# A distance table repeated from memory to memory between weight tiles, and narrow columns loaded apart from the stream

## The chip, the cores and the metric

The kernel runs on one core of one Trainium2 chip. The metric is the device time of one execution in microseconds (us), as the median of several runs. All times below come from one profiled execution of the kernel before, except where "runs" are named. Engines are PE (matrix multiply), ACT, DVE and POOL (elementwise work), SP (which only issues transfers here), and 16 DMA engines that all queues share.

## The reference

Two transformer blocks in float32 on 256 tokens of width 2048, one after the other. The first block has modulated attention, pooling and a feed-forward of width 8192. The second has four attention branches, a gate for each, and an output projection. What matters here is the end of the first block and the start of the second:

```python
hm = modulate(rms_norm(x, norm_mlp_w), sh_m, sc_m)
x = x + g_m * squared_relu_mlp(hm, w_mlp_up, w_mlp_down)   # feed-forward
...
h = rms_norm_2(x, norm_w)
p = h @ w_in                       # (2048, 17492)
(z, gate, dsa_qkv, idx_q, idx_k, idx_w, fox_qkv, fox_f, diff_qkv, dil_qkv) = jnp.split(p, IN_OFFSETS, axis=-1)
bias_dsa, bias_diff, bias_dil = jnp.split(rel_bias, 3, axis=-1)   # rel_bias: (32, 12)
...
bias = bias_table[t5_bucket(tq[:, None] - key_pos[None, :])].transpose(2, 0, 1)
logits = jnp.where(causal, logits + bias[None, :, None], -jnp.inf)
```

Three of the branches add a bias to their logits that depends only on the distance of query and key and on the head: 3 branches of 4 heads, 12 rows in all. `idx_k` (64 columns), `idx_w` (16) and `fox_f` (4) are the narrow columns of `p`: 84 of them, of which 80 lie side by side.

## The kernel before, in words

**Weights as a stream.** Every weight is read once, in tiles of 1 MB (512 rows by 512 columns). The order is written out by hand as a list of items (L278 to L381). `issue` (L127) takes the next item, finds a free buffer `raw` (three of them, and two more up to the second quarter of the feed-forward, L396) and starts its transfer on SP's queue (L148). What `with_issue` holds for an item is called just before that item's own transfer (L142). `prep` (L157) splits half a tile at a time: ACT rounds it to `wh` (L65, called from L172) and DVE forms the rest `wl` (L68). There are five buffers of each. `take` (L222) hands a half-tile to PE and lets `prep` run three half-tiles ahead. When both halves of a tile are split, its buffer is free and the next transfer is issued. PE does three products for each step of 128 rows and each half of the tokens (L231 to L233): 12 for a half-tile.

**Small work in between.** After each half-tile `tick` (L94) takes one step of the queue `hp` and, by `lp_rate`, steps of the queue `lp`. These are generators with the small work of the stage: transposes, norms, attention.

**Feed-forward.** Four quarters `c` (L1003). Each has 16 tiles of `w_mlp_up` and then 16 of `w_mlp_down`. Beside the up tiles of `c` = 1 and 2 run 12 tiles of `w_ada` that DVE multiplies and sums into `g_part` (L177 to L190), and no `lp` work is left in this stage. The item of the first down tile of `c` = 1 is `down_blk[1, 0][0]`, and the 16 down items have numbers that follow each other.

**Between the blocks.** The pool `b1` of the first block is closed and `b2` is opened at the same place in memory (L1043 to L1046). A tile of `b2` waits only for the tiles of `b1` whose bytes it takes (`reuse_waits="tile"`). The first tiles of `b1` were `crows` (512 bytes of each partition) and the two extra `raw` buffers (8 KB each). The second of these became `g_part`, which is read to the end of the feed-forward. The other carries weights for the last time in `c` = 0. A tile with tag `T` of `b2` takes 4 KB, and there are two.

On POOL's queue then come, in this order: the factor of the norm (L485), four pieces of the norm's row (L1052), the table `c2`, `relb`, `bucket_hot` and `dist_mask` (the last two into a `T` tile `hv`), and seven small transfers (L1092 to L1099). `tables` (L1103), a generator in `hp`, multiplies `relb` by `hot` on PE (L1105), adds the mask on DVE (L1107) and issues one transfer on POOL's queue: 12 rows of 383 numbers, in 12 partitions, each written 128 times to `dist_bias` in memory (L1108). `bias_tile` (L1122) later reads from there, for each branch, rows that are shifted by one from partition to partition. This runs beside the projection of the first branch (`qkv("dsa")`).

**The narrow columns** are item `sm` of the stream (L370), after the tiles of the first branch: one item of 16 steps of 128 rows by 84 columns, fetched by two transfers into one `raw` buffer, in pieces of 320 and of 16 bytes. PE uses it at L1472 to L1474.

```python
it = items[i]
if i in with_issue:
    with_issue.pop(i)()
if it[0] == "w":
    ...
    for src, c0, c1 in parts:
        nc.sync.dma_start(v[:, :, c0:c1], src.rearrange("(k p) n -> p k n", p=128))
```

Of the kernel before, what the change touches and what calls it, by code (L numbers as in the profile page):

```python
# [17 lines left out]
T = 256  # L18
# [4 lines left out]
# tiles of weights on their way: always, and more in the first block  # L23
RAW, RAW_EXTRA = 3, 2
# where the second input is loaded in the order of the weights
CTX_AT = "u0"
# tiles of the modulation: before the feed-forward, in the input projection, beside each half of the output projection
FILL, ADA_IN, ADA_POOL, ADA_REST = 4, 10, 4, 1
# background steps beside the output projection; steps by which queries and keys are turned later than they are projected
LP1, LAG, LAGK = 1.1, 3, 2  # L30
# background steps beside each branch of the second block
RATES = (1.2, 1.2, 1.2, 1.0)

# columns of the constant table of the first block
C1_COS, C1_SIN, C1_SEL, C1_N = 0, 128, 256, 258
# columns of the constant table of the second block
C2_TRI, C2_CNT, C2_CAUSAL, C2_SCORE, C2_N = 0, 256, 512, 768, 1024
# columns of the second block's input projection
# [4 lines left out]
def two_blocks_kernel(ctx: ExitStack, tc: tile.TileContext, I, out: bass.AP):  # L43
# [83 lines left out]
    def issue():  # L127
        i = state["issued"]
        if i >= len(items):
            return  # L130
        if i < extra["until"] and extra["live"] < RAW_EXTRA:
            extra["live"] += 1
            from_extra.add(i)
            r = extra["pool"].tile([128, 2048], FP32, tag="raw", name="raw", bufs=RAW_EXTRA)
        elif extra["main"] < RAW:
            extra["main"] += 1
            r = raw_p.tile([128, 2048], FP32, tag="raw", name="raw")
        else:
            return
        state["issued"] += 1  # L140
# [4 lines that stand above are left out]
            _, parts, kt, n = it  # L145
            v = r[:, 0:kt * n].rearrange("p (k n) -> p k n", k=kt)
            for src, c0, c1 in parts:
                nc.sync.dma_start(v[:, :, c0:c1], src.rearrange("(k p) n -> p k n", p=128))  # L148
            raws[i] = v
        elif it[0] == "ak":  # L150
            raws[i] = r[:, 0:4 * it[3].shape[1]].rearrange("p (k n) -> p k n", k=4)
            nc.sync.dma_start(raws[i], it[3].rearrange("(k p) n -> p k n", p=128))
        else:
            raws[i] = r.rearrange("p (k n) -> p k n", k=4)
            nc.sync.dma_start(r, it[3])

    def prep():  # L157
# [8 lines left out]
        if it[0] == "w":  # L166
# [4 lines left out]
            src = r[:, h * kh:(h + 1) * kh, :]  # L171
# [5 lines left out]
        elif it[0] == "av":  # L177
            # this part's share of the row, by partition
            _, key, k, _ = it
            rf = r.rearrange("p k n -> p (k n)")  # L180
            c = cst[:, k, 0:1]
            if not g_part:
                g_part.append(extra["pool"].tile([128, 2048], FP32, tag="raw", name="g_part", bufs=RAW_EXTRA))
                V.tensor_scalar(g_part[0], rf, c, None, op0=OP.mult)
            else:
                for h_ in range(2):
                    s_ = slice(1024 * h_, 1024 * h_ + 1024)
                    V.scalar_tensor_tensor(out=g_part[0][:, s_], in0=rf[:, s_], scalar=c, in1=g_part[0][:, s_],
                                           op0=OP.mult, op1=OP.add)
            done = True  # L190
        else:
            # four products at a time, each in 32 columns of the array
            kind, key, k, _ = it
            n_k = 4 if kind == "ak" else FILL if key == ("g", 5) else 16
            n = r.shape[2]
            if k == 0:
                accs[key] = bank([128, n], "adab", "ada")
            for j in range(4):
                PE.matmul(out=accs[key][32 * j:32 * j + 32, :], lhsT=cst[:, 4 * k + j if kind == "ak" else k, :],  # L199
                          rhs=r[:, j, :], start=k == 0, stop=k == n_k - 1)  # L200
            if k == n_k - 1:
                rows = b1.tile([128, 512], FP32, tag="rows", name="rows", bufs=2)[:, 0:n]
                act(rows, accs.pop(key))
                after_item[key[0]](rows, *key[1:])
            done = True
        if done:
            raws.pop(i)
            extra["live" if i in from_extra else "main"] -= 1
            issue()
# [77 lines left out]
    # groups of the rows of w_in, in steps of 128; the first are short for an early start  # L287
# [55 lines left out]
    # two blocks of columns, whose groups of rows come in an order of their own  # L343
# [23 lines left out]
    for nm, c0, nb in (("dsa", DSA0, 3), ("sm", 0, 0), ("idx", IDXQ0, 2), ("fox", FOX0, 3), ("diff", DIFF0, 3),  # L367
                       ("dil", DIL0, 3), ("z", Z0, 4)):
        if nm == "sm":
            in2["sm"] = [add_w("w", [(w_in2[:, IDXK0:IDXK0 + 80], 0, 80), (w_in2[:, FOXF0:FOXF0 + 4], 80, 84)], 16, 84)]  # L370
        else:
            if nm == "dsa":
                in2["dsa", 0] = pair_w(w_in2, 0, c0, c0 + 512, LATE)
            for j in range(2 if nm == "dsa" else 0, nb):
                in2[nm, j] = w_block(w_in2, 0, c0 + 512 * j)
# [53 lines left out]
    # bias of the gates of the residual, in the rows where their products land  # L429
# [17 lines left out]
    # silu of both conditions, the stationary operand of the modulation  # L447
# [33 lines left out]
    # reciprocal root of the mean of squares  # L481
# [36 lines left out]
    # scaled per partition, split in two parts  # L518
# [4 lines left out]
    # scaled and shifted per column, split in two parts  # L523
# [125 lines left out]
    # turned by the position, in place but for the last sum; each head twice, side by side  # L649
# [127 lines left out]
    # a unit: one head, half of the tokens; two heads of the same tokens follow each other  # L777
# [93 lines left out]
    # rows of the pooling branch, beside the attention  # L871
# [24 lines left out]
    # rows of the attention  # L896
# [40 lines left out]
    hm_hi, hm_lo = [], []  # L937

    # the norm's factor of each token, in all partitions
# [61 lines left out]

    fh = lhs_of(hm_hi, hm_lo)
    for c in range(4):  # L1003
        if c == 1:
            V.tensor_tensor(out=gb[5], in0=g_rows[5], in1=gb[5], op=OP.add)
# [41 lines left out]

    def wt(shape, name="w"):
# [35 lines left out]
    relb = b2.tile([32, 12], FP32, name="relb", bufs=1)  # L1084
    G.dma_start(relb, I["rel_bias_2"])
    hv = b2.tile([128, 2, 512], FP32, tag="T", name="hv")
    hot, vmask = hv[:, 0], hv[:, 1]
    G.dma_start(hot[0:32, 0:384], I["bucket_hot"])
    G.dma_start(vmask[0:12, 0:384], I["dist_mask"])
# [10 lines left out]
    dist_bias = dram.tile([12, 128, 383], FP32, name="dist_bias")  # L1100
    lam = b2.tile([128, 4], FP32, name="lam", bufs=1)

    def tables():  # L1103
        bk = bank([128, 384], "bias")
        PE.matmul(out=bk[0:12, :], lhsT=relb, rhs=hot[0:32, 0:384], start=True, stop=True)  # L1105
        vec = vmask[0:12, 0:384]
        V.tensor_tensor(out=vec, in0=bk[0:12, :], in1=vec, op=OP.add)  # L1107
        G.dma_start(dist_bias, bc(vec[:, None, 0:383], [12, 128, 383]))  # L1108
        yield
# [73 lines left out]
    # names: attention whose operands must be gone first  # L1183
# [137 lines left out]
    def fox(f_nat):  # L1321
# [8 lines left out]
        # log(1 + u) = 2 artanh(u / (2 + u))  # L1330
# [44 lines left out]
    def diff():  # L1375
# [32 lines left out]
        def sixth(u, pt):  # L1408
# [4 lines left out]
            # a sum of squares past the largest float32 makes the reference's reciprocal root 0  # L1413
# [51 lines left out]
    # few columns: the weights stand still, the tokens move  # L1465
# [144 lines left out]
    # the last rows of the last block: one half of the tokens first  # L1610
# [22 lines left out]
def _constants():  # L1633
# [9 lines left out]
    # keys of the other block: within 128 positions, or far below any score  # L1643
# [28 lines left out]
    # distance 255 - m in column m  # L1672
# [32 lines left out]
```

## Time and profile before

| | |
|---|---|
| runs (3) | median 2212.37 us, 2210.87 to 2212.54 |
| profiled execution, first to last instruction (span) | 2209.1 us |
| what lies around the span | 3.3 us, by the median; the page gives no time of its own for the profiled execution |
| PE busy | 2141.7 us, 97% |
| DVE, ACT, POOL busy | 55%, 44%, 1% |
| read and written by DMA | 468.9 MB, 212 GB/s on average |
| granted clock of PE | 0.987 of full speed on average |

Every row of the trace has its start in us from the first instruction. A row of a chain or a timeline gives the start, how long it took, the engine and line, and `output<-input`. Brackets give how long the engine had been idle before it and what released it. A matmul's own time (0.39 us) is longer than its share of PE's time, because the next one starts before it ends; the distance of two starts is what counts. "DMA share" is the mean busy share of the 16 DMA engines; q1 is the queue of SP's transfers and q0 that of POOL's.

### The profile page before, as it was taken

What the parts mean: (1) busy time and instruction counts of PE and PEld (TensorE: products, weight loads), DVE (VectorE), ACT (ScalarE), POOL (GpSimd) and SP (SyncE); (2) the same over time, 40 slices, a digit from 0 to 9 for tenths busy, and PEclk for the clock granted to TensorE, in tenths of its full rate; (3) what the DMA queues carried; (4) which work ended last, traced back from release to release, by engine and by line L of the source; (5) the groups of instructions that cost most, each with busy time, mean ns of one, the idle gap of its engine ahead of it and who ended that gap; (6) DMA issues with size and microseconds to landing.
All of it is one profiled execution on the core that took longest, in us unless ns stands there. A gap on an engine that the chain in (4) does not pass through costs nothing.

```text
span 2209.1 us, 25697 instructions
## 1 busy us (share of the span) xinstructions
PE 2141.7 (97%) x10291; PEld 1694.4 (77%) x10291; DVE 1220.0 (55%) x1552; ACT 973.4 (44%) x1355; POOL 33.0 (1%) x59
## 2 busy tenths in 40 slices
PE   6899999999999999999999889999999999999998
PEld 3566655678888888888888777888888888888886
DVE  2455655555546646554456447756665555555554
ACT  4433344355444434434444444445544444444443
POOL 1000000000000000000001000000000000000000
PEclk8999999999999999999999999999999999999999
DMA  9988876665547667556545764444546555555553
GB/s 332 325 313 335 316 285 235 236 226 195 202 160 279 229 208 249 193 188 198 183 153 190 187 216 153 162 170 155 181 169 214 197 189 196 189 197 189 193 191 114
DMA packets 215703, 468.90 MB, mean 212 GB/s; under 512 B 12472, under 2 KB 21148, under 8 KB 206624
## 3 DMA queue, kind: packets, MB, share of 16 engines
q1 hardware_dynamic: 211712, 455.86, 59.6%
q0 software_dynamic: 3408, 11.17, 2.2%
q8 instruction: 80, 1.31, 0.2%
q14 instruction: 39, 0.32, 0.0%
q10 hardware_dynamic: 464, 0.24, 0.0%
HBM read 462.79 MB, written 4.45 MB: 212 GB/s over the span
## 4 chain that ended last, share of the span: by engine, by line
PE 81%; issue 13%; DMA 3%; ACT 1%; DVE 1%; POOL 0%; ACTq 0%; POOLq 0%; SPq 0%; DVEq 0%
PE acc L231 26%; PE acc L233 25%; PE acc L232 25%; DMA raw<-in_w_in_dram 2%; PE adab L199 1%; DMA raw<-in_w_ada_dram 1%; PE bk L979 1%; PE s L1200 1%; ACT v L65 1%; PE o L1243 0%; PE bk L1290 0%; ACT wh L65 0%; PE bk L1519 0%; PE bk L1144 0%; DMA vrows<-in_norm_attn_w_dram 0%
## 5 line engine op out<-in xcount | busy, mean ns | idle before, releaser
L68 DVE TENSOR_TENSOR wl<-raw,wh 128x1024 fp32r<-128x1024 f32 (+2 forms) x676 | 801.1, 1205 | 626.5 <-ACT wh L65 626.2
L65 ACT ACTIVATE wh<-raw 128x1024 fp32r<-128x1024 f32 (+2 forms) x676 | 693.2, 1044 | 534.6 <-PE acc L233 442.9
L231 PE MATMUL acc<-wh,xX 128*128 128x512 f32 x1888 | 759.4, 402 | 12.9 <-ACT wh L65 11.6
L233 PE MATMUL acc<-wh,xX 128*128 128x512 f32 x1888 | 738.9, 391 | 0.0
L232 PE MATMUL acc<-wl,xX 128*128 128x512 f32 x1888 | 738.2, 391 | 0.5 <-DVE wl L68 0.5
L231 PEld LDWEIGHTS acc<-wh,xX 128*128 128x128 f32 x1888 | 356.4, 189 | 109.5 <-issue 21.5
L233 PEld LDWEIGHTS acc<-wh,xX 128*128 128x128 f32 x1888 | 355.9, 189 | 76.6 <-DVE xX L68 0.2
L232 PEld LDWEIGHTS acc<-wl,xX 128*128 128x128 f32 x1888 | 356.9, 189 | 71.0 <-issue 1.2
L231 PE MATMUL acc<-wh,xR 128*128 128x512 f32 x704 | 280.8, 399 | 4.1 <-DVE xX L629 2.2
L233 PE MATMUL acc<-wh,xR 128*128 128x512 f32 x704 | 275.1, 391 | 0.0
L232 PE MATMUL acc<-wl,xR 128*128 128x512 f32 x704 | 274.8, 390 | 0.0
L231 PEld LDWEIGHTS acc<-wh,xR 128*128 128x128 f32 x704 | 132.5, 188 | 35.0 <-issue 3.8
L233 PEld LDWEIGHTS acc<-wh,xR 128*128 128x128 f32 x704 | 132.5, 188 | 28.1 <-DVE xR L68 0.2
L232 PEld LDWEIGHTS acc<-wl,xR 128*128 128x128 f32 x704 | 132.8, 189 | 27.4 <-issue 1.4
L199 PE MATMUL adab<-raw,cst 128*32 128x512 f32 (+1 forms) x736 | 92.2, 599 | 15.9 <-DMA raw<-in_w_ada_dram 9.8
L199 PEld LDWEIGHTS adab<-raw,cst 128*32 128x32 f32 x736 | 17.6, 113 | 54.0 <-issue 28.0
L65 ACT ACTIVATE p<-s,negm 128x512 f32<-128x512 f32 x32 | 22.1, 690 | 52.1 <-DVE negm L792 32.3
L65 ACT ACTIVATE g<-acc,r 128x512 f32<-128x512 f32 x30 | 20.6, 691 | 55.5 <-PE acc L233 55.5
L65 ACT ACTIVATE xR<-bk 128x512 f32<-128x512 f32 (+2 forms) x26 | 13.9, 534 | 66.2 <-PE bk L1144 29.9
L65 ACT ACTIVATE r<-acc 128x512 f32<-128x512 f32 x32 | 19.0, 600 | 52.2 <-PE acc L233 41.3
L65 ACT ACTIVATE junk<-x 128x512 f32<-128x512 f32 x32 | 20.3, 633 | 48.7 <-DVE x L1586 22.6
L65 ACT ACTIVATE v<-bk 128x512 f32<-128x512 f32 x32 | 19.3, 602 | 45.7 <-PE bk L979 45.7
(285 smaller groups left out, 1299.9 us busy)
## 6 DMA issues: line engine op xcount, KB each, us to landing
raw<-in_w_in_dram SPq DMA_DIRECT2D x151, 1024.0 KB, 4.9
raw<-in_w_ada_dram SPq DMA_DIRECT2D x88, 1024.0 KB, 6.5
raw<-in_w_mlp_up_dram SPq DMA_DIRECT2D x64, 1024.0 KB, 5.3
raw<-in_w_mlp_down_dram SPq DMA_DIRECT2D x64, 1024.0 KB, 5.1
raw<-in_w_out_dram SPq DMA_DIRECT2D x32, 1024.0 KB, 5.2
raw<-in_w_branch_dram SPq DMA_DIRECT2D x16, 1024.0 KB, 5.1
raw<-in_w_ada_dram SPq DMA_DIRECT2D x16, 512.0 KB, 8.1
raw<-in_w_in_dram SPq DMA_DIRECT2D x10, 512.0 KB, 6.5
```

What stands on the lines that cost most here:

```text
L65: S.activation(out=out_, in_=in_, func=func, **kw)
L68: V.tensor_tensor(out=lo, in0=full, in1=hi.bitcast(FP32), op=OP.subtract)
L199: PE.matmul(out=accs[key][32 * j:32 * j + 32, :], lhsT=cst[:, 4 * k + j if kind == "ak" else k, :], rhs=r[:, j, :], start=k == 0, stop=k = ...
L231: PE.matmul(out=acc, lhsT=hi, rhs=wh, start=first, stop=False)
L232: PE.matmul(out=acc, lhsT=hi, rhs=wl, start=False, stop=False)
L233: PE.matmul(out=acc, lhsT=lo, rhs=wh, start=False, stop=last)
L979: PE.transpose(bk[:, j, t * 128:(t + 1) * 128], rs[t][:, (2 * pr + j) * 128:(2 * pr + j + 1) * 128], ident)
L1200: PE.matmul(out=s[:, i, :], lhsT=QT[nm][p, h, t * 128:(t + 1) * 128], rhs=KT[nm][p, h, 0:nk], start=True, stop=True)
```

## The change

The diff, without the comments it also takes out:

```diff
@@ issue, prep
+        if items[i][1] is None:
+            raws[i] = ahead_of(i)
+            state["issued"] += 1
+            return issue()
...
-            src = r[:, h * kh:(h + 1) * kh, :]
+            src = r[h] if parts is None else r[:, h * kh:(h + 1) * kh, :]
...
         if done:
             raws.pop(i)
+            if it[1] is None:
+                return
             extra["live" if i in from_extra else "main"] -= 1
             issue()
@@ order of the stream
-            in2["sm"] = [add_w("w", [(w_in2[:, IDXK0:IDXK0 + 80], 0, 80), (w_in2[:, FOXF0:FOXF0 + 4], 80, 84)], 16, 84)]
+            in2["sm"] = [add_w("w", None, 16, 84)]
...
+    narrow = []
+
+    def ahead_of(i):
+        return narrow
@@ feed-forward
+    relb = const.tile([32, 12], FP32, name="relb")
+    dist_row = dram.tile([12, 383], FP32, name="dist_row")
+    dist_bias = dram.tile([12, 128, 383], FP32, name="dist_bias")
+
+    def dist_tables():
+        G.dma_start(relb, I["rel_bias_2"])
+        hot, vec = (b1.tile([128, 512], FP32, tag="rm", name=nm) for nm in ("hot", "vec"))
+        G.dma_start(hot[0:32, 0:384], I["bucket_hot"])
+        G.dma_start(vec[0:12, 0:384], I["dist_mask"])
+        for _ in range(8):
+            yield
+        bk = bank([128, 384], "bias")
+        PE.matmul(out=bk[0:12, :], lhsT=relb, rhs=hot[0:32, 0:384], start=True, stop=True)
+        vec = vec[0:12, 0:384]
+        V.tensor_tensor(out=vec, in0=bk[0:12, :], in1=vec, op=OP.add)
+        for _ in range(2):
+            yield
+        G.dma_start(dist_row, vec[:, 0:383])
+        yield
+
+    def repeat(h):
+        def f():
+            nc.sync.dma_start(dist_bias[h], bass.AP(tensor=dist_row.tensor, offset=dist_row.offset + h * 383, ap=[[0, 128], [1, 383]]))
+        return f
+
+    for h in range(12):
+        with_issue[down_blk[1, 0][0] + h] = repeat(h)
...
         if c == 1:
+            lp.append(dist_tables())
@@ start of the second block, ahead of everything else in b2
+    for h in range(2):
+        narrow.append(b2.tile([128, 8, 84], FP32, tag="T", name="narrow"))
+        for c0, n, at in ((IDXK0, 80, 0), (FOXF0, 4, 80)):
+            G.dma_start(narrow[h][:, :, at:at + n], w_in2[1024 * h:1024 * h + 1024, c0:c0 + n].rearrange("(k p) n -> p k n", p=128))
...
-    relb = b2.tile([32, 12], FP32, name="relb", bufs=1)
-    G.dma_start(relb, I["rel_bias_2"])
-    hv = b2.tile([128, 2, 512], FP32, tag="T", name="hv")
-    hot, vmask = hv[:, 0], hv[:, 1]
-    G.dma_start(hot[0:32, 0:384], I["bucket_hot"])
-    G.dma_start(vmask[0:12, 0:384], I["dist_mask"])
...
-    dist_bias = dram.tile([12, 128, 383], FP32, name="dist_bias")
...
     def tables():
-        bk = bank([128, 384], "bias")
-        PE.matmul(out=bk[0:12, :], lhsT=relb, rhs=hot[0:32, 0:384], start=True, stop=True)
-        vec = vmask[0:12, 0:384]
-        V.tensor_tensor(out=vec, in0=bk[0:12, :], in1=vec, op=OP.add)
-        G.dma_start(dist_bias, bc(vec[:, None, 0:383], [12, 128, 383]))
-        yield
```

The 12 rows are now made in the second quarter of the feed-forward (`c` = 1) and written once to `dist_row` in memory. From there 12 transfers on SP's queue, of 128 rows of 1532 bytes each (196 KB), read one row 128 times and write it to `dist_bias`, from memory to memory. Each is issued just before one of the first 12 down tiles of `c` = 1. The narrow columns are fetched by four transfers on POOL's queue, two for each half of the rows, into two `T` tiles of their own. The stream passes over their item: it takes no `raw` buffer and no transfer on SP's queue.

## Rows read from the trace of the kernel before

**Rows 1.** The page: span, PE, and the chain that ended last, by engine.

```profile
span 2209.1 us, 25697 instructions
PE 2141.7 (97%) x10291; PEld 1694.4 (77%) x10291; DVE 1220.0 (55%) x1552; ACT 973.4 (44%) x1355; POOL 33.0 (1%) x59
...
PE 81%; issue 13%; DMA 3%; ACT 1%; DVE 1%; POOL 0%; ACTq 0%; POOLq 0%; SPq 0%; DVEq 0%
```

**Rows 2.** Waits, 1195 to 1340 us: total us, times, longest us.

```profile
POOL T L1124 <- DMA dist_bias<-hv: 32.9, 1, 32.9
ACT wh L65 <- DMA raw<-in_w_in_dram: 25.6, 5, 18.9
...
PE acc L231 <- ACT wh L65: 11.6, 1, 11.6
```

**Rows 3.** The chain in order of time, 1235 to 1280 us: start, us.

```profile
1239.46 0.76 PE bias L1105 x2
...
1240.71 1.20 DVE wl L68
...
1241.94 32.52 DMA raw<-in_w_in_dram
...
1274.55 1.07 ACT wh L65
```

**Rows 4.** POOL in order of time, 300 to 1590 us.

```profile
474.50 2.00 POOL L437 DMA_DIRECT2D gb<-in_b_ada_dram  x4 [0.29 <-POOL gb L434]
...
1205.83 0.72 POOL L485 TENSOR_TENSOR rs<-rs,half_neg 128x2 f32<-128x2 f32 x1 [729.32 <-DVE rs L484]
...
1241.08 1.17 POOL L1108 DMA_DIRECT2D dist_bias<-hv  x1 [5.24 <-DVE hv L1107]
1275.18 0.78 POOL L1124 DMA_DIRECT2D T<-dist_bias  x1 [32.92 <-DMA dist_bias<-hv]
1395.89 0.75 POOL L1124 DMA_DIRECT2D T<-dist_bias  x1 [119.93 <-DVE L L1209]
```

**Rows 5.** DMA queues, 1255 to 1270 us: packets, MB, share of 16 engines.

```profile
q0 software_dynamic: 245, 1.13, 67.0%
q1 hardware_dynamic: 244, 0.50, 8.4%
```

**Rows 6.** PE in order of time, 1260 to 1281 us.

```profile
1260.27 0.60 PE L1144 MATMUL bk<-ident,n 128*128 128x128 f32 x4
...
1262.54 0.39 PE L233 MATMUL acc<-wh,xX 128*128 128x512 f32 x1
...
1263.45 0.60 PE L1144 MATMUL bk<-ident,n 128*128 128x128 f32 x4
1275.66 0.79 PE L231 MATMUL acc<-wh,xX 128*128 128x512 f32 x1 [11.61 <-ACT wh L65]
...
1280.03 0.39 PE L233 MATMUL acc<-wh,xX 128*128 128x512 f32 x1
```

**Rows 7.** Stretches: busy us of PE, PEld, DVE, ACT, POOL; PE clock, DMA share, GB/s.

```profile
657.00:746.00 89.00, 89.00 (x407) 73.75 (x406) 61.13 (x58) 40.02 (x46) 0.00 (x0) 1.00 0.78 274
746.00:835.00 89.00, 89.00 (x398) 73.76 (x397) 47.60 (x45) 37.03 (x37) 0.00 (x0) 1.00 0.60 200
690.00:700.00 10.00, 10.00 (x46) 8.29 (x45) 7.80 (x7) 2.10 (x3) 0.00 (x0) 1.00 0.98 343
...
1275.66:1280.00 4.34, 3.87 (x8) 2.76 (x9) 3.90 (x5) 2.80 (x4) 0.30 (x1) 0.50 1.08 281
```

**Rows 8.** SP's transfers in order of time, 640 to 900 us.

```profile
727.23 0.37 SPq L148 DMA_DIRECT2D raw<-in_w_mlp_up_dram  x1
733.69 74.15 SPq L148 DMA_DIRECT2D raw<-in_w_mlp_down_dram  x16
```

**Rows 9.** PE in order of time, 681 us.

```profile
681.56 0.60 PE L979 MATMUL bk<-ident,r 128*128 128x128 f32 x4
```

**Rows 10.** ACT in order of time, 788 to 792 us.

```profile
788.80 1.06 ACT L65 ACTIVATE wh<-raw 128x1024 fp32r<-128x1024 f32 x1 [1.66 <-PE acc L233]
791.52 1.06 ACT L65 ACTIVATE wh<-raw 128x1024 fp32r<-128x1024 f32 x1 [1.66 <-PE acc L233]
```

**Rows 11.** Waits, 640 to 900 us.

```profile
ACT wh L65 <- DMA raw<-in_w_mlp_up_dram: 25.9, 11, 4.3
```

**Rows 12.** DMA issues of the whole run: KB each, median us to landing.

```profile
raw<-in_w_mlp_down_dram SPq DMA_DIRECT2D x64, 1024.0 KB, 5.1
...
dist_bias<-hv POOLq DMA_DIRECT2D x1, 2298.0 KB, 33.8
```

**Rows 13.** DMA traffic, 1275 to 1280 us.

```profile
DMA packets 3298, 1.38 MB, mean 275 GB/s; under 512 B 2896, under 2 KB 2896, under 8 KB 3298
...
q1 hardware_dynamic: 3154, 0.85, 73.2%
```

**Rows 14.** DMA queue of POOL, 1205 to 1212 us, with the pieces of one row.

```profile
q0 software_dynamic: 159, 0.52, 39.1%
```

## The prediction

> **What bounds the kernel now.** I read the page first. PE is busy 97% of the span and holds 81% of the chain that ended last [rows 1], so a change pays only where PE stands still, or where its stalls could be made longer. The waits around the end of the first block come next: there is one large stall of PE, 11.61 us in front of a product of the weight stream. It waits for ACT's `wh`, and ACT had waited 18.9 us for a weight tile [rows 2]. The chain in order of time shows that tile: issued at 1241.94, it landed 32.52 us later [rows 3], where a weight tile takes 5.1 us in the median [rows 12]. POOL's timeline gives the neighbour: the transfer `dist_bias<-hv` was issued at 1241.08 [rows 4] and took 33.8 us [rows 12]. The two ran side by side.
>
> The DMA queues between 1255 and 1270 show how. POOL's queue gave 245 packets with 1.13 MB, so 4.6 KB each, three rows of 1532 bytes. SP's queue gave 244 packets of 2 KB [rows 5]. They alternate one by one. A packet of POOL's took 0.670 x 16 x 15 / 245 = 0.66 us of an engine, one of SP's 0.084 x 16 x 15 / 244 = 0.083 us. A weight tile is 512 pieces of 2 KB, 32 for each engine, so it needs 32 x 0.74 = 24 us beside that transfer. PE's lead over the stream was used up before that.
>
> **What the stall costs.** Four transposes start at 1260.27 and the ninth product after them at 1262.54, so 2.27 us later. The same four start at 1263.45, and there the ninth product after them starts at 1280.03 [rows 6]. Without the stall it would start at 1263.45 + 2.27 = 1265.72. The loss is 14.3 us: PE's idle time, the wait for `wl`, and eight products at half clock (0.50, the 1.2 GHz level, until 1280 [rows 7], after 11.61 us of idleness).
>
> **The change, part by part.**
>
> *The transfer from SBUF goes.* With it goes its contention, and the tile of 1241.94 should land after 5.1 us, at 1247, against a product at 1263.8 that needs it. Gain: 14.3 us. Next late there is nothing that the waits show [rows 2]; PE would run through.
>
> *Twelve repeats on SP's queue.* Memory to memory appears nowhere in the trace of before. A repeat is 128 rows, 196 KB. From below: POOL's queue, loading pieces of one row into many partitions among other things, used 0.391 x 16 x 7 = 43.8 us of an engine for 0.52 MB [rows 14], so 0.084 us for a KB and 16 us for a repeat: 1.0 us on 16 engines. From above: the transfer of before divided by twelve, 33.8 / 12 = 2.8 us. I take the price of a row there, 0.66 / 3 = 0.22 us, by 8 rows for each of 16 engines: 1.8 us. It has the same row length and the same target.
>
> The room for it: from 746 to 835, the second half of quarter 1, 16 tiles take 89 us, 5.56 us each, at a DMA share of 0.60 [rows 7]. So 2.2 us of each are free, and 1.0 or 1.8 us fit. With 2.8 us the stream falls behind by 0.6 us a tile, 7 us after twelve. That is covered too: ACT starts a half-tile each 2.72 us, when PE lets go of the buffer five before it [rows 10], and PE comes to it four half-tiles later, 10.9 us; the split takes 1.06 us on ACT [rows 10] and 1.20 us on DVE [rows 3], so `wl` is 8.6 us early. The three `raw` buffers add to that: they come round in 6 x 2.72 = 16.3 us, of which landing (5.1) and splitting both halves (2.72 + 2.3) need 10.1, so 6.2 us are spare. Cover: 14.8 us. Cost: nothing, as long as a repeat stays under 2.2 + 14.8 / 12 = 3.4 us. If that cover is gone, the price is 12 us for each further us of a repeat.
>
> Here a rule weighs on the choice between the bounds. The row: the SBUF transfer moved 1.13 MB in 15 us, 75 GB/s, at 67% of the engines [rows 5]. The Trainium skill, page "SBUF — State Buffer", section on the DMA port swizzle, says that bandwidth goes by how many of 16 ports the partitions reach, 27.2 GB/s each; 12 partitions reach three, an estimate of 82 GB/s by that page, and the trace agrees. By that rule the slowness belonged to the source and a repeat from memory would run at the pace of weights, an estimate of half a us each; the sum stays the same, and the chance of dear repeats becomes smaller.
>
> *The wait on SP.* The first repeat waits for `dist_row`, and every weight tile is queued behind it on SP. The first transposes of quarter 1, which the first tick after its first half-tile of block `n` = 1 issues, stand at 681.56 [rows 9]; that is the ninth tick, the one that issues the bias product. The product (0.76 us [rows 3]) and DVE's add follow at once, so `dist_row` can be issued near 683. The first repeat comes after the transfer of 727.23 [rows 8]. Even a landing as slow as 33.8 us would be in time. SP's issues cost 0.37 us each [rows 8], on an engine that mostly waits.
>
> *Product, add and loads of the table.* They move from the second block into quarter 1, the same number on PE and DVE: nothing. The three loads go to POOL while it stands idle, from 476.5 to 1205.8 [rows 4].
>
> *The narrow columns on POOL's queue.* Four transfers, 4096 pieces. They take the first 8 KB of `b2`, that is `crows` and the extra `raw` buffer that is not `g_part`, both free since quarter 0. So they leave right behind `dist_row`, near 685, beside the up tiles of quarter 1 (DMA share 0.78, so 22% of 89 us free [rows 7]). Price: from 1275 to 1280 SP's queue gave 3154 packets, 2896 of them under 512 bytes, in 0.732 x 16 x 5 = 58.6 us of engines [rows 13]. The other 258, at 0.083 us, take 21.4, which leaves 12.8 ns for a small piece: 52 us, 3.3 us on 16 engines. From above, all 58.6 put on the small ones: 20 ns, 5.2 us. From below nothing, if they fill the gaps. The longest that ACT waits there for a tile is 4.3 us [rows 11], and PE never stands still [rows 7], so of the 8.6 us at least 4.3 are left. I take 3.3 us: covered. At 5.2 us, 0.9 us of PE time would show.
>
> *What is moved past.* At the start of the second block POOL's queue loses three loads, so the rest lands earlier. The read back of the table need not wait 32.9 us any more [rows 4]; it now waits for a `T` tile, until the first narrow half is split. The next such read waits for DVE's use of the first one and is issued at 1395.89 [rows 4], so the first one has about 100 us. The stream loses one item on SP and one `raw` turn: a gain in cover, none in time.
>
> **Sum.** Span 2209.1 - 14.3 = 2194.8 us. The page has no total of the profiled execution; the median of the runs lies 3.3 us above the span, so 2198.1 us.
>
> **Rivals.**
>
> 1. *The narrow pieces delay the up tiles.* At twice my price, 6.6 us against 4.3 left, and with some us at half clock after a stall, PE loses 2 to 5 us: 2200.5 to 2203. For it: the DMA share reaches 0.98 from 690 to 700 [rows 7], and packets of POOL's queue alternate with the weights one by one [rows 5]. Against it: [rows 13] shows many of them going through in 5 us beside weights. The Trainium skill, page "DMA: Bandwidth & Descriptors", section "Issuing engines are not separate DMA queues", speaks against this part: all queues share the 16 engines, so loading outside the stream frees none of them. The trace agrees (245 packets to 244 in [rows 5]); by that rule the bytes are still paid for, and only where they fall decides.
>
> 2. *Slower: the 128 reads of one row go one at a time.* Place: SP's queue in the down tiles of quarter 1. A repeat then takes 128 x 0.084 x 1.5 = 16 us; twelve fall behind by 12 x (16 - 2.2) = 166 us, less 14.8 of cover: 2198 + 151 = 2349 us. It decides from 3.4 us a repeat; from 2.2 + (14.8 + 14.3) / 12 = 4.6 us on the kernel is slower than before. Against it: in [rows 14] 39% of 16 engines, six at once, were reading pieces that for the most part come from few rows.
>
> 3. *No change.* Repeats of 4 to 5 us bring the same 14 us of stall to quarter 1: about 2212. Or the change does not do what it says, because the tile of 1241.94 is late for another reason. Against it: the alternation and its pace account for 24 us of the 32.5, and both ends match.
>
> **Numbers.** My forecast gets 0.80, rival 1 0.10, rival 2 0.05, rival 3 0.05. Forecast alone: 2196 to 2200 (1 us for runs, as they spread by 1.7; 1 us for narrow pieces at their upper bound). The range takes in rival 1 and leaves out the other two: 2195.8 to 2203.5. Of rival 3's chance 0.01 falls on either side of 0.2% (4.4 us, about what a measurement of this kernel can tell from no change), 0.03 inside. Faster 0.80 + 0.10 + 0.01 = 0.91, same 0.03, slower 0.05 + 0.01 = 0.06.
>
> **What would show it.** Right: no idle PE of over 1 us between 1200 and 1300, clock 1.00 there, weight tiles landing in 5 to 7 us; twelve `dist_bias<-dist_row` on SP's queue between about 728 and 800, each landing within some 5 us; four loads of `narrow` near 685; PE busy the whole of both halves of quarter 1. Wrong: ACT waiting for down tiles of quarter 1 and PE after it (rival 2 or 3); PE idle near 690 to 710 (rival 1); a tile that is still late near 1242.

## The result, and the profile after

| | kernel before | changed kernel |
|---|---|---|
| runs, taken side by side | median 2211.62 us (2210.41 to 2212.54, 4 runs) | median 2195.3 us (2194.07 to 2198.57, 4 runs) |
| profiled execution, span | 2209.1 us | 2193.6 us, in a run of 2195.33 us |

The ratio is 0.9932, with a 95% interval of 0.992 to 0.9944: faster by 0.68%. On the median of 2212.37 us shown ahead of the prediction that is 2197.3 us, where 2198.1 us was forecast. The median of 2195.3 us itself lies 0.5 us below the low end of the range. These two medians are of runs taken side by side; the experiments below have their own runs of the kernel before beside them, and their ratios are the numbers to compare.

The page of the changed kernel, the lines of [rows 1]:

```profile
span 2193.6 us, 25721 instructions
PE 2136.0 (97%) x10291; PEld 1690.6 (77%) x10291; DVE 1220.6 (56%) x1552; ACT 970.9 (44%) x1355; POOL 35.9 (2%) x63
...
PE 83%; issue 13%; DMA 2%; ACT 1%; DVE 1%; POOL 0%; ACTq 0%; POOLq 0%
```

PE's only wait from 600 to 1340 us (total, times, longest); in [rows 2] there was one of 11.6 us:

```profile
PE bk L1325 <- ACT rel L65: 0.2, 1, 0.2
```

Stretches, as in [rows 7]. PE is busy through the place of the old stall, at full clock, and through both halves of quarter 1. There the DMA share has risen from 0.78 to 0.84 and from 0.60 to 0.68:

```profile
657.00:746.00 89.00, 89.00 (x403) 72.98 (x402) 61.18 (x59) 37.88 (x45) 4.13 (x5) 1.00 0.84 282
746.00:835.00 89.00, 89.00 (x398) 73.70 (x397) 48.99 (x47) 37.07 (x37) 0.00 (x0) 1.00 0.68 224
...
1255.00:1270.00 15.00, 15.00 (x80) 12.71 (x79) 6.17 (x7) 6.50 (x9) 0.80 (x1) 1.00 0.43 142
```

Weight tiles issued between 1235 and 1290 us, time to landing (min, median, max); before, the longest was the 32.5 us of [rows 3]:

```profile
DMA to landing us min/median/max: 4.8/4.9/5.3
```

POOL in order of time, as in [rows 4]. The 12 rows of the table leave at 682, the narrow columns right behind them, and the read back at 1261 now waits for a `T` tile (DVE's `wl`), not for the table:

```profile
473.70 2.01 POOL L449 DMA_DIRECT2D gb<-in_b_ada_dram  x4 [0.29 <-POOL gb L446]
...
682.17 0.52 POOL L1032 DMA_DIRECT2D dist_row<-vec  x1 [204.95 <-DVE vec L1029]
683.08 3.61 POOL L1094 DMA_DIRECT2D narrow<-in_w_in_dram  x4 [0.39 <-issue]
1205.11 0.73 POOL L497 TENSOR_TENSOR rs<-rs,half_neg 128x2 f32<-128x2 f32 x1 [518.42 <-DVE rs L496]
...
1261.05 0.80 POOL L1159 DMA_DIRECT2D T<-dist_bias  x1 [24.73 <-DVE wl L68]
1380.14 0.76 POOL L1159 DMA_DIRECT2D T<-dist_bias  x1 [118.30 <-DVE L L1244]
```

SP in order of time, as in [rows 8]: the first, second and last repeat.

```profile
725.97 0.37 SPq L152 DMA_DIRECT2D raw<-in_w_mlp_up_dram  x1
726.39 0.57 SPq L1038 DMA_DIRECT2D dist_bias<-dist_row  x1
732.22 0.37 SPq L152 DMA_DIRECT2D raw<-in_w_mlp_down_dram  x1
732.64 0.51 SPq L1038 DMA_DIRECT2D dist_bias<-dist_row  x1
...
779.32 0.51 SPq L1038 DMA_DIRECT2D dist_bias<-dist_row  x1
```

DMA issues, as in [rows 12] (KB each, median us to landing):

```profile
dist_bias<-dist_row SPq DMA_DIRECT2D x12, 191.5 KB, 6.6
...
narrow<-in_w_in_dram POOLq DMA_DIRECT2D x2, 320.0 KB, 4.4
...
narrow<-in_w_in_dram POOLq DMA_DIRECT2D x2, 16.0 KB, 3.7
```

ACT's waits for weight tiles, 640 to 900 us. The longest for an up tile was 4.3 us in [rows 11]; waits for down tiles are new. PE felt none of them.

```profile
ACT wh L65 <- DMA raw<-in_w_mlp_up_dram: 29.0, 10, 5.9
...
ACT wh L65 <- DMA raw<-in_w_mlp_down_dram: 6.6, 2, 3.8
```

### The profile page after: what moved, and what is told of

Read it like the earlier page. It is cut to its first block, busy times and chain, and to the rows that moved or that the text cites. A ratio compares the mean times of both kernels' runs of the same rounds, so it can differ in the third digit from the quotient of the medians.

```text
span 2193.6 us, 25721 instructions
## 1 busy us (share of the span) xinstructions
PE 2136.0 (97%) x10291; PEld 1690.6 (77%) x10291; DVE 1220.6 (56%) x1552; ACT 970.9 (44%) x1355; POOL 35.9 (2%) x63
## 4 chain that ended last, share of the span: by engine, by line
PE 83%; issue 13%; DMA 2%; ACT 1%; DVE 1%; POOL 0%; ACTq 0%; POOLq 0%
PE acc L237 26%; PE acc L239 26%; PE acc L238 26%; DMA raw<-in_w_ada_dram 1%; PE adab L203 1%; PE bk L991 1%; PE s L1235 1%; ACT v L65 1%; PE o L1278 0%; PE bk L1179 0%; PE bk L1325 0%; PE bk L1554 0%; ACT wh L65 0%; DMA c<-in_c_dram 0%; PE colb L557 0%
## 5 line engine op out<-in xcount | busy, mean ns | idle before, releaser
L68 DVE TENSOR_TENSOR wl<-raw,wh 128x1024 fp32r<-128x1024 f32 (+1 forms) x674 | 799.6, 1207 | 607.3 <-ACT wh L65 607.0
L65 ACT ACTIVATE wh<-raw 128x1024 fp32r<-128x1024 f32 (+1 forms) x674 | 690.3, 1043 | 517.8 <-PE acc L239 443.5
```

The source lines that it names most:

```text
L65: S.activation(out=out_, in_=in_, func=func, **kw)
L68: V.tensor_tensor(out=lo, in0=full, in1=hi.bitcast(FP32), op=OP.subtract)
```

## The experiments

The change has three parts at once: another source (memory for SBUF), another place and size (twelve pieces in quarter 1), and the narrow columns taken out of the stream. The first runs take them apart. In each code cut "..." stands for lines left out.

**The table alone.** The narrow columns are back in the stream:

```diff
-            in2["sm"] = [add_w("w", None, 16, 84)]
+            in2["sm"] = [add_w("w", [(w_in2[:, IDXK0:IDXK0 + 80], 0, 80), (w_in2[:, FOXF0:FOXF0 + 4], 80, 84)], 16, 84)]
-    for h in range(2):
-        narrow.append(b2.tile([128, 8, 84], FP32, tag="T", name="narrow"))
-        ...
```

> The changed kernel with the narrow columns put back into the stream as before; only the table is made early and repeated from memory. Theory 1 (the stall came from the transfer out of SBUF alone, the narrow item had no part in it): 2195 to 2197 us, no idle PE of over 1 us between 1200 and 1300. Theory 2 (the narrow item's 4096 pieces on SP's queue were part of the stall): 2 to 6 us slower than the changed kernel, with ACT waiting for a weight tile behind the narrow item near 1255 to 1265.

Measured: 2197.46 us, ratio to the kernel before 0.9934 (0.9921 to 0.9948), the same as the changed kernel's 0.9932 within the intervals. The median is 2.2 us above that of the changed kernel, which by itself would fit the low end of theory 2. But the profiled execution was already 2.2 us later at 475.87 us, where the changed kernel's stands at 473.70, ahead of anything that differs. From there to the mark on POOL near 1550 us (the factor `rsd`, shown further down) it takes 1075.4 us, the changed kernel 1075.5. PE never waits between 600 and 1340 us, and ACT's one wait for a weight tile between 1195 and 1340 is 3.1 us long, against 2.6 in the changed kernel. Theory 1 holds.

Without the narrow columns beside them, ACT's waits for up tiles are:

```profile
ACT wh L65 <- DMA raw<-in_w_mlp_up_dram: 28.4, 10, 4.5
```

With them the longest goes from 4.5 to 5.9 us, each in one execution. What the narrow columns cost the engines can be read from POOL's queue in the changed kernel, 682 to 690 us (packets, MB, share):

```profile
q0 software_dynamic: 288, 0.71, 36.8%
```

That is 0.368 x 8 = 2.9 us of all 16 engines, with the small transfer to `dist_row` (32 of the packets) in it. The 4096 pieces were moved here in 256 packets.

**The narrow columns alone.** The table is made and repeated as in the kernel before; `hot` and the mask sit in other buffers, since `narrow` holds both `T` tiles:

```diff
+    hot, vmask = (b2.tile([128, 512], FP32, tag="pt", name=nm) for nm in ("hot", "vmask"))
...
+        G.dma_start(dist_bias, bc(vec[:, None, 0:383], [12, 128, 383]))
```

> The kernel before with only the narrow columns loaded apart; the table stays one transfer from SBUF on POOL's queue near 1241 us. Theory 1: the tile issued near 1242 still lands some 30 us later and PE still idles 8 to 12 us: 2208 to 2212 us. Theory 2: a stall shorter by half or more: 2198 to 2205 us.

Measured: 2209.52 us, ratio 0.9994 (0.9985 to 1.0002). The stall stands, with a tile that took 32.1 us to land; PE's wait in this run:

```profile
PE acc L237 <- ACT wh L65: 11.1, 1, 11.1
```

So the narrow columns are not what the change gains.

**The old transfer at the new place.** The one transfer out of SBUF, in quarter 1:

```diff
-        G.dma_start(dist_row, vec[:, 0:383])
+        G.dma_start(dist_bias, bc(vec[:, None, 0:383], [12, 128, 383]))
-    for h in range(12):
-        with_issue[down_blk[1, 0][0] + h] = repeat(h)
```

> The changed kernel, but with the one transfer from 12 partitions of SBUF (as before) issued at the new place near 682 us, instead of 12 repeats from memory. Theory 1 (what makes the stall is how that transfer alternates with the weights, wherever it stands): a weight tile near 690 takes over 20 us, and PE idles 8 to 25 us between 690 and 730: 2205 to 2222 us. Theory 3 (the new place alone is what helps, because the stream has more in hand in the feed-forward): 2195 to 2198 us.

Measured: 2220.65 us, ratio 1.0039 (1.0025 to 1.0053), slower than before the change. PE's wait:

```profile
PE acc L237 <- ACT wh L65: 21.3, 1, 21.3
```

and the stretch that holds it, with PE busy for 67 us of 89:

```profile
657.00:746.00 89.00, 67.27 (x290) 54.11 (x289) 44.66 (x44) 25.34 (x29) 4.88 (x5) 0.87 0.84 226
```

A weight tile took 33.5 us to land there. The new place is the worse one for that transfer. The likely reason, not tested apart, is that the stream is denser there: a DMA share of 0.78 in [rows 7], with the tiles of `w_ada`, against 0.43 in the changed kernel at the old place. Theory 3 falls: earlier does not mean hidden.

**The new source at the old place.** One transfer of 2.3 MB on POOL's queue near 1244 us, read from memory:

```diff
-        G.dma_start(dist_bias, bc(vec[:, None, 0:383], [12, 128, 383]))
+        G.dma_start(dist_row, vec[:, 0:383])
+        G.dma_start(dist_bias, bass.AP(tensor=dist_row.tensor, offset=dist_row.offset, ap=[[383, 12], [0, 128], [1, 383]]))
```

> The kernel before, with the table at its old place and still one transfer of 2.3 MB on POOL's queue, but read from 12 rows in memory instead of 12 partitions of SBUF. Theory 1 with the source as the cause of the slow rows: 0.1 us or less for a row instead of 0.22, landing within 18 us instead of 33.8, and the stall shrinks to 0 to 3 us: 2196 to 2201 us. Theory 4 (the bulk of 2.3 MB in one piece is what hurts, whatever it is read from; twelve pieces between the tiles are needed): PE still idles 8 us or more: 2207 to 2213 us.

Measured: 2196.38 us, ratio 0.9936 (0.9922 to 0.9949): the whole gain, without twelve pieces, without the new place and with the narrow columns in the stream. PE's longest wait there is 0.3 us. The transfer landed after 18.2 us instead of 33.8. Its packets between 1248 and 1258 us (packets, MB, share), to be held against [rows 5]:

```profile
q0 software_dynamic: 334, 1.54, 74.9%
```

A packet of 4.6 KB takes 0.749 x 16 x 10 / 334 = 0.36 us of an engine, 0.12 us a row, where [rows 5] gave 0.66 and 0.22. The row and the landing just miss what theory 1 asked (0.1 us and 18 us); the time and the stall are as it said. Theory 4 falls. The source decides.

**Out of SBUF, but from spread partitions.** Is it SBUF as such, or twelve neighbours in it? The 12 rows lie in partitions 0, 4, ... 28 and 64 to 76 in steps of 4; POOL's queue, old place:

```diff
-        G.dma_start(dist_bias, bc(vec[:, None, 0:383], [12, 128, 383]))
+        G.dma_start(dist_bias[0:8], bc(vmask[0:32:4, None, 0:383], [8, 128, 383]))
+        G.dma_start(dist_bias[8:12], bc(vmask[64:80:4, None, 0:383], [4, 128, 383]))
```

> The kernel before, with the table still repeated out of SBUF at its old place on POOL's queue, but the 12 rows in partitions 0, 4, ... 28 and 64, 68, 72, 76 instead of 0 to 11, in two transfers (8 and 4 rows). Theory 5 (the slow rows come from neighbouring partitions that share a way out of SBUF): a packet of three rows takes 0.4 us or less instead of 0.66, landing within 20 us, PE idles under 3 us: 2196 to 2202 us. Theory 6 (reading one partition again and again is slow by itself, wherever it lies): 0.6 us or more a packet, and PE idles 8 us or more: 2207 to 2214 us. The Trainium skill, page SBUF - State Buffer, section on the DMA port swizzle, has partitions 0 to 11 on three of sixteen ports and these twelve on twelve of them; it stands with theory 5.

Its partner makes the same two transfers from partitions 0 to 7 and 8 to 11:

```diff
+        G.dma_start(dist_bias[0:8], bc(vec[0:8, None, 0:383], [8, 128, 383]))
+        G.dma_start(dist_bias[8:12], bc(vec[8:12, None, 0:383], [4, 128, 383]))
```

> The partner of the run with spread partitions: the same two transfers of 8 and 4 rows out of SBUF, from partitions 0 to 7 and 8 to 11 as before. Theories 5 and 6 alike: as slow as before, landing of the first near 33 us or less by a little, PE idle 8 to 14 us, 2207 to 2214 us. If the split in two transfers was what helped, it would be as fast as the spread one, 2196 to 2202 us.

Measured: spread 2195.1 us, ratio 0.9927 (0.991 to 0.9943), just under the range of theory 5; side by side 2211.3 us, ratio 1.0004 (0.9995 to 1.0013). POOL's queue between 1246 and 1254 us from spread partitions:

```profile
q0 software_dynamic: 586, 1.54, 58.3%
```

and side by side:

```profile
q0 software_dynamic: 357, 0.65, 67.6%
```

PE's wait in the kernel with the rows side by side; the spread one's longest there is 0.2 us:

```profile
PE acc L231 <- ACT wh L65: 12.4, 1, 12.4
```

A KB takes 0.583 x 16 x 8 / 1540 = 0.048 us of an engine from spread partitions and 0.676 x 16 x 8 / 650 = 0.133 us from neighbours: 0.07 and 0.20 us a row of 1.5 KB, the latter near the 0.22 of [rows 5]. So neither SBUF as such, nor the bulk, nor the moment made the stall, but twelve rows side by side. This agrees with the Trainium skill, page "SBUF — State Buffer", section on the DMA port swizzle: the bandwidth of a transfer goes by how many of the 16 ports its partitions reach. The spread rows differ in two things, the step of four partitions and the use of both halves of SBUF; which of them is needed was not tried. A change of a dozen lines in one place thus gives all of the gain of the change; the two differ by less than their spread.

**How much the cover bears.** Each repeat is issued two, three or six times, into tables that nobody reads (one, two or five more of them):

```diff
+    more = [dram.tile([12, 128, 383], FP32, name=f"more{i}") for i in range(2)]
...
-            nc.sync.dma_start(dist_bias[h], ...)
+            for d in (dist_bias, *more):
+                nc.sync.dma_start(d[h], ...)
```

> The changed kernel with each of the twelve repeats issued twice. Three times cost 13.5 us of span and six times 92 us, so a repeat's price in the packed stream lies between (13.5 + 14.8 + 26.4) / 36 = 1.5 us and (92 + 14.8 + 26.4) / 72 = 1.85 us, against a cover that ends at 3.4 us for each tile. Two of them, 3.0 to 3.7 us: at or just under that edge, 0 to 4 us lost: 2195 to 2199 us. If the busy share's 1.0 us held, nothing lost and ACT never waiting for a down tile by more than in the changed kernel (3.8 us). If the cover is smaller than reckoned: 5 to 9 us lost.

> The changed kernel with each of the twelve repeats issued three times (two more copies of the table that nobody reads). A repeat costs 1.0 us of 16 engines by the changed kernel's DMA share in the second half of quarter 1 (0.68 against 0.60 over 89 us, seven repeats). Theory 1 with my cover (2.2 us free a tile, 14.8 us in hand): 12 x (3.0 - 2.2) = 10 us behind, covered: no idle PE there, 2195 to 2198 us. If a repeat holds up the weights for its 6.4 us to landing and not for its share of the engines: 12 x (19 - 2.2) - 15, over 150 us slower.

> The changed kernel with each of the twelve repeats issued six times (five more copies that nobody reads). Theory 1: 12 x (6.1 - 2.2) - 14.8 = 32 us of PE time lost in the down tiles of quarter 1: 2220 to 2235 us. With the 1.8 us a repeat that the forecast had taken: 12 x (10.8 - 2.2) - 14.8 = 88 us, about 2284 us. If the cover is much larger than reckoned: under 2210 us.

Measured: twice 2194.13 us (0.9923, 0.9906 to 0.9939), three times 2206.3 us (0.998, 0.997 to 0.9989), six times 2288.06 us (1.0355, 1.0337 to 1.0373). The second half of quarter 1 in that order, each in its own kernel's trace:

```profile
746.00:835.00 89.00, 89.00 (x398) 73.65 (x397) 49.50 (x48) 36.63 (x36) 0.00 (x0) 1.00 0.78 256
```

```profile
746.00:835.00 89.00, 81.70 (x343) 63.89 (x342) 40.41 (x40) 32.40 (x34) 0.00 (x0) 0.98 0.86 256
```

```profile
746.00:835.00 89.00, 52.10 (x160) 37.89 (x161) 19.87 (x20) 16.07 (x18) 0.00 (x0) 0.74 0.90 165
```

Two repeats a tile are free; ACT's longest wait for a down tile grew from 3.8 to 4.5 us, and PE felt none of it. Three cost 11 us by the medians (13.5 us of span, 2207.1 against 2193.6, in the profiled execution, the slowest of its ten). Six cost 92 us (2285.8). Theory 1 expected nothing at three and 32 us at six: wrong at both.

The price of a repeat is not fixed. Its packets are rows of 1532 bytes, and nothing else on SP's queue has that size, so the trace tells them apart. In the mean one takes 0.076 us of an engine in the changed kernel, 0.091 with two repeats a tile, 0.125 with three and 0.187 with six. A repeat of 128 rows is thus 0.6, 0.7, 1.0 and 1.5 us of all 16 engines. The 1.0 us on which the expectations for three and six rest was its price at three, not in the changed kernel; the 1.5 to 1.85 expected for two was twice what it was. With the measured prices the reckoning gives 12 x (3.0 - 2.2) - 14.8, nothing, at three and 12 x (9.0 - 2.2) - 14.8 = 67 us at six, still less than was lost. The 88 us by 1.8 us a repeat came near at six, but the same price would give 12 x (5.4 - 2.2) - 14.8 = 24 us at three.

SP's own waits show what the reckoning by busy share left out, here with three repeats, 727 to 800 us:

```profile
SPq L1041 <- DMA more<-dist_row: 14.1, 15, 1.9
SPq L152 <- DMA raw<-in_w_mlp_down_dram: 10.0, 7, 2.1
...
SPq L1041 <- DMA dist_bias<-dist_row: 5.0, 4, 1.8
```

SP itself waits for earlier transfers to land before it issues the next, 29 us in this stretch. In the changed kernel these waits come to 0.2 us, and SP waits instead for buffers to come free (53.9 us there, 8.2 with three).

An estimate from rows says how this eats the cover. Counted from the first repeat, the eleventh down tile is issued 15.3 us later with three repeats than in the changed kernel (795.13 - 727.30 against 778.89 - 726.39). Down tiles issued from 725 to 800 land after 12.6 us in the median, against 6.2. Together that is 21.7 us, 6.9 more than the 14.8 of cover, and PE's waits there add up to 7.1 us. By this estimate the cover was about as large as reckoned, and what the reckoning left out is that issue and landing get slower. Which of the two counts for more, and how many transfers may be under way, was not tried.

## Why the prediction was right, point by point

**What bounds the kernel; the stall's cause.** Right. The tile of 1241.94 was late because its packets alternated with those of the transfer out of SBUF. The runs that keep the transfer out of neighbouring partitions (narrow columns alone, new place, side by side) keep a stall of 11 to 21 us beside it; those that don't (table alone, from memory, spread) have none: PE's longest wait there is 0.3 us. That part of rival 3 which doubted the cause is refuted.

**The size of the gain.** Forecast 14.3 us, from two sequences of products in [rows 6]. A later mark on POOL gives the measure, the factor `rsd` of the third branch. Before:

```profile
1564.89 1.04 POOL L485 TENSOR_TENSOR rsd<-rsd,half_neg 128x4 f32<-128x4 f32 x1 [168.25 <-DVE rsd L484]
```

and after:

```profile
1549.19 1.03 POOL L497 TENSOR_TENSOR rsd<-rsd,half_neg 128x4 f32<-128x4 f32 x1 [168.28 <-DVE rsd L496]
```

From the norm's factor (1205.83 in [rows 4], 1205.11 after) to there, 359.06 us became 344.08: 15.0 us. The stall gave back what was reckoned and 0.7 us more, which no row assigns. The 0.7 us by which the norm's factor itself comes earlier are no gain: POOL's four transfers of `gb` already start 0.8 us earlier (474.50 in [rows 4], 473.70 after), ahead of everything that was changed, and over the experiments that place varies from 471.85 to 475.87.

**The sum.** One term was mis-sized: "what lies around the span", 3.3 us, was the median of the runs less the span of another execution. The changed kernel's own pair is 2195.33 - 2193.6 = 1.7 us. That is 1.6 us; the span was 2193.6 against 2194.8 forecast. Together these put the median 2.8 us below the forecast and just under the range. In the ratio the term drops out: 2212.37 - 2197.3 = 15.1 us against the 14.3 forecast.

**Twelve repeats.** Covered, as forecast, but mis-sized. By their packets they cost 0.6 us each of all engines: under the lower bound of 1.0, and a third of the 1.8 that I took. The DMA share alone misleads here. It gives (0.68 - 0.60) x 89 = 7.1 us for the eight repeats whose packets fall into that stretch, 0.9 us each, but the stretch also moved 24 GB/s more, 2.1 MB, of which eight repeats are only 1.6; the rest are weights that happen to fall into it. With these taken off, 1.4 us at 0.083 us for 2 KB, 0.7 us are left. By the port rule of the Trainium skill's page "SBUF — State Buffer", section on the DMA port swizzle, I had estimated half a us for a repeat, at the pace of weights. The trace agrees in the main: 0.6 us in the mean, and 0.065 us a row, 0.5 us a repeat, in the median.

Two signs were off. Each repeat was to land within some 5 us; the median is 6.6. And the edge was put at 3.4 us a tile by busy share alone, but three repeats, 3.0 us by their packets, lay under it and lost 11 us, since transfers were issued and landed later. With one repeat a tile, neither mattered.

**The wait on SP.** Right: `dist_row` left at 682.17 us (forecast near 683), the first repeat followed the transfer of 725.97 and had not to wait.

**The narrow columns.** Right in place (683 us), covered, and near in price: 2.9 us of the engines against 3.3 taken, by luck in part, since the price of a small piece came from SP's queue and POOL's moved larger packets. The longest wait grew by 1.4 us, as rival 1 had it in kind, but of the 8.6 us reckoned there 2.7 were left. The columns brought no time: in the stream they cost nothing measurable, apart from it neither.

**Rivals 2 and 3.** Repeats did not go one at a time: 0.6 us of the engines each and 6.6 us to landing, where rival 2 had 16 us. Nor did they bring a stall to quarter 1, as rival 3 had it. The edge is between two and three repeats a tile.

## What to carry to other kernels

When a weight stream stalls beside a bulk transfer, compare the engine time of a packet on the two queues before asking how many bytes move: 0.66 us against 0.083 us, alternating, made a 5 us tile take 32. Rows that are read many times out of SBUF should lie apart (every fourth partition, in both halves, was enough here), or go by way of memory; moving the same transfer to another place moved the stall with it, and made it longer. Judge how many small transfers fit between tiles by trying two and three of them, not by the free share of the engines. And take the price of a transfer from its own packets: the share of a stretch also counts whatever else falls into it.

## What the runs showed of the hardware that was not expected

- The same 12 rows, written the same way out of SBUF: 0.20 us a row and landing after 35.5 us at the latest from partitions 0 to 11, 0.07 us a row and 16.2 us from partitions four apart in both halves of SBUF.
- A row read 128 times from memory, in one transfer of twelve rows on POOL's queue (0.12 us), is dearer than one from spread partitions, and cheaper than one from neighbours. In twelve transfers on SP's queue it took 0.076 us.
- That price rises with the number under way: 0.091, 0.125 and 0.187 us a row with two, three and six repeats a tile.
- With three or six repeats a tile SP waited for the landing of earlier transfers, 29 us in 73 us with three and 51 in 143 with six, while the engines' share stood at 0.88 and 0.90.
